# Two more pairs of tiles as seven block products, and input scaling and low parts moved to GpSimd, in a two-layer hybrid trunk

## The chip, the cores and the metric

The kernel runs on one core of a Trainium2 chip. The metric is device time in microseconds (us) from one launch; what is compared is the median of several runs. The profile names the engines PE (TensorE, with PEld for its weight loads), DVE (VectorE), ACT (ScalarE), POOL (GpSimd) and SP (SyncE, which here only issues DMA).

## The reference, cut to what matters

Two layers over 528 tokens (16 learned ones ahead of 512), width 1024, all in float32:

```
h = RMSNorm(x)
[u_pool | z_pool | c_q | c_kv | k_rope | z_mla | g_pool | g_mla] = h @ W_in
y_pool = (pool_mix(u_pool) * silu(z_pool)) @ W_pool_up
y_mla  = (attention(c_q, c_kv, k_rope) * silu(z_mla)) @ W_mla_up      8 heads, causal, q and k normalised, rotary part
x = x + (sigmoid(g_pool) * y_pool + sigmoid(g_mla) * y_mla) @ W_out
```

The 16 learned tokens are dropped at the end, so the second layer computes most things for 512 tokens only. The change touches, in the second layer, the columns of `W_in` that give `z_mla` (tiles `zm0` to `zm3`, 128 columns each), `g_pool` (`gp0` to `gp7`) and `g_mla` (`gm0` to `gm7`).

## The kernel before

**Precision.** Matmuls run in a reduced float32 format. To keep float32 accuracy each operand is split into a high part (ScalarE copies it into the reduced format) and a low part (VectorE subtracts the high part from the original). A product is three matmuls, `mm3`, lines 187 to 193: high by high (L188), high by low (L191), low by high (L192). `split`, lines 294 to 296, does it for activations; `wload`, lines 173 to 185, for weights, which come from HBM in chunks of 128 x 512 (K = 512 rows of a tile of 128 columns). A chunk costs a DMA on SP, an ACT copy (L183, `whi`) and a DVE subtraction (L184, `wlo`). There are three buffers each for the raw chunk, the high part and the low part.

**The stream.** `register` lists all weight products of both layers in order, as `Gemm` entries in `plan`; `stream` walks that list and yields after every few matmuls, with their nominal time. `clk` adds up these nominal times. `go` writes out the remaining work of a layer (norms, softmax, attention) and between its steps calls `fill`, `fill_now`, `fill_to` or `upto`, which take so many nominal nanoseconds of matmuls from the stream, or all up to a named entry. `after` puts a piece of work on a list that is run when `clk` has passed a given time. So the attention's small steps are covered by the stream's matmuls. In the second layer `gap` fills 2,700 nominal ns and stops at the entry in `RESERVE` ("gm5"), so that later entries are left to cover the end of the last head. The framework then orders each engine's instructions by a simulated timeline, so the order in the trace can differ from the program's.

**Block products.** `fast`, lines 599 to 646, computes two neighbouring tiles (a pair) as one 2 x 2 product of blocks: two halves of K by two tiles, times two halves of K by two halves of 256 tokens, with seven block products in place of eight (Winograd's form). Each of the seven is 4 k-steps x 3 matmuls of 256 columns. It needs sums of activation blocks, made by `mixed` (lines 577 to 597) on DVE and ACT once for all pairs, and sums of weight blocks, which `weight_sums` (lines 339 to 355) makes in the first layer: copies from HBM to HBM on SP's queue, additions by accumulating DMA on GpSimd's queue, four sums a pair, kept in `wsum`. The results come out of four PSUM banks through one ACT copy and five DVE additions or subtractions, then through `got_gp`, which applies the gate. Before, the four pairs of `gp` are made so.

**Plain entries.** `zm0` to `zm3` (`ev_zm`, lines 556 to 565) and `gm0` to `gm7` (`ev_gate`, lines 1029 to 1035) are plain: 8 k-steps x 3 matmuls of 512 columns. `ev_zm` makes one tanh on ACT and one instruction on DVE (L562), `ev_gate` one tanh; the gates `gm0` to `gm5` are stored to HBM and fetched again later.

**Input scaling.** `renorm`, lines 566 to 575, scales each of eight blocks of 128 rows of the layer's input by its gain and by the inverse norm (L573, on DVE), and splits it in place of the unscaled one. Blocks 0 to 3 are loaded from HBM first, since their buffer is in use. `qk_stats` calls it for the blocks in the order 4, 5, 6, 7, 0, 1, 2, 3, with 1,500 nominal ns of fill after each. `zm0` is the first entry that reads the scaled input.

**Heads.** For each of eight heads, `prep` (lines 840 to 860) multiplies keys by their inverse norm (DVE for one half, L847; GpSimd for the other, L848), splits keys (`kh`, `kl`) and queries (`qh`, `ql`, L854 and L855), and copies rotary parts by DMA. `head` computes scores, maxima (L877, DVE), exponentials (L884, ACT), and the normalisation by the row sums on GpSimd (L922, L924). `pv` transposes and multiplies by the values, one head later (L944 to L950). `go` calls `mixed` three times a head in the second layer, until its eight steps are done.

Of the kernel before, what the change touches and what calls it, by code (L numbers as in the profile page):

```python
# [53 lines left out]
RESERVE = ("gm5", "gm5")  # L54
# [4 lines left out]
SPACE = 4500.0  # L59
# [13 lines left out]
def trunk(ctx, tc, xT, pos, win, wkr, wqb, wkb, wvb, wgr, wpu, wmu, wout, gains, const, yT):  # L73
# [220 lines left out]
    def split(hi, lo, src, a, b):  # L294
        act.activation(hi[:, a:b], src, AF.Copy)  # L295
        dve.tensor_sub(lo[:, a:b], src, hi[:, a:b].bitcast(F32))  # L296
# [33 lines left out]
    wsum = [dp.tile([P, 4, 512], F32, name=f"wsum{u}") for u in range(4)]  # L330
# [8 lines left out]
    def weight_sums(w):  # L339
        def made(u, i):  # L340
            a, b = w[2 * u], w[2 * u + 1]
            d = wsum[u]
            src = {0: (b[:, 0:512], b[:, 512:1024]), 2: (a[:, 0:512], b[:, 0:512]), 1: (a[:, 0:512], d[:, 0, :]),
                   3: (a[:, 512:1024], d[:, 1, :])}
            return d[:, i, :], src[i]

        def copy(d, src):
            behind(sp.dma_start(d, src[0]), earlier(9000))

        def add(d, src):  # L350
            behind(gp.dma_start(d, src[1], accum_op=ALU.add), earlier(4000))

        for u in range(4):
            for fn, i in ((copy, 0), (copy, 2), (add, 0), (copy, 1), (add, 2), (add, 1), (copy, 3), (add, 3)):
                yield lambda fn=fn, u=u, i=i: fn(*made(u, i))

    class Layer:
        def __init__(self, l):
# [12 lines left out]
            self.f, self.tt, self.part = [None] * 8, [None] * 4, {}  # L371
            self.st = self.acc = self.inv = self.cinv = self.kraw = self.kp = None
# [193 lines left out]
        def renorm(self, k):  # L566
# [3 lines left out]
            if k < 4:  # L570
                sp.dma_start(f, scr[:, k, :])
                x = f
            behind(dve.scalar_tensor_tensor(out=f, in0=x, scalar=self.g(G_H + k), in1=self.inv[:, NM:T],  # L573
                                            op0=ALU.mult, op1=ALU.mult), newest[0])
# [24 lines left out]
        def fast(self, name, a, b, u, got):  # L599
# [4 lines left out]
            bank = {}  # L604

            def body(i, w):
# [21 lines left out]
                elif p == 5:  # L628
                    dve.tensor_sub(v, v, ps)
                    got(2 * u + 1, XH[1], v, v)  # L630
                elif p == 2:
                    got(2 * u, XH[0], ps, tmp()[:, :N2])
                elif p == 4:
                    x = tmp()[:, :N2]
                    dve.tensor_sub(x, ps, d)
                    got(2 * u + 1, XH[0], x, x)
                else:
                    dve.tensor_add(d, d, ps)
                    got(2 * u, XH[1], d, d)
# [6 lines left out]
        def got_gp(self, m, s, v, t):  # L646
            am = self.am[m][:, s[0]:s[1]]
            act.activation(t, v, AF.Tanh, scale=0.5)
            dve.scalar_tensor_tensor(out=am, in0=t, scalar=1.0, in1=am, op0=ALU.add, op1=ALU.mult)

# [154 lines left out]
        def qk_stats(self):  # L805
# [34 lines left out]
        def prep(self, h):  # L840
# [9 lines left out]
            split(kh, kl, kf[:, :T], 0, T)  # L850
# [4 lines left out]
            dve.tensor_sub(ql[n0:n0 + 64, x0:T], src, qh[n0:n0 + 64, x0:T].bitcast(F32))  # L855
# [218 lines left out]
        def register(self, nxt):  # L1074
# [46 lines left out]
            for m in range(4):  # L1121
                add(f"zm{m}", wi(MT_ZM + m), D, evac=self.ev_zm(m) if self.last else self.ev_silu(self.zms, "u", m),
                    xs=hs, segs=XS)
            if self.last:
                for e in ("gm0", "gm1", "gp0", "gm2", "gp1", "gm3", "gp2", "gm4", "gp3", "gm5", "gm6", "gm7"):
                    m = int(e[2])
                    if e[:2] == "gp":
                        self.fast(e, wi(MT_GP + 2 * m), wi(MT_GP + 2 * m + 1), m, self.got_gp)
                    else:
                        add(e, wi(MT_GM + m), D, evac=self.ev_gate(m), xs=hs, segs=XS)  # L1130
# [16 lines left out]
        def go(self, nxt):  # L1147
# [145 lines left out]
```

## Time and profile before

| | before |
|---|---|
| median of 3 runs | 788.73 us (788.3 to 789.17) |
| the profiled execution, whole | 788.28 us |
| its span, first to last instruction | 786.4 us |
| instructions | 15094 |
| granted TensorE clock | 1.000 of full speed |
| DMA, mean over the span | 124 GB/s |
| HBM read, written | 88.64 MB, 14.23 MB |

The profile is one execution. The page gives busy time by engine, the span in 40 slices with the busy share in tenths (9 is 90% or more), the chain of work that ended last, followed backwards from the last instruction, and groups of instructions: line, engine, operation, what is written and read, shapes, count, then busy time and mean nanoseconds of one, then idle time of the engine just before them and what ended it. A line like L184 is a line of the kernel. Matmuls overlap, so their durations add up to more than the time they take; starts are what to compare. Views of the trace give the same for a stretch of time (windows), for a line, or instruction by instruction (timeline: start, duration, engine, line, what).

### The profile page before, as it was taken

To read this page: it belongs to the slowest core of one execution; us is meant where nothing else is said; L and a number is where in the kernel's file an instruction comes from. 1 tells how busy PE (TensorE), PEld (TensorE's weight loads), DVE (VectorE), ACT (ScalarE), POOL (GpSimd) and SP (SyncE) were. 2 spreads that over 40 slices of the span, in tenths; PEclk is the share of its full clock that TensorE was granted. 3 is DMA by queue.
4 is the path that set the end of the run, shared out by engine and by line. 5 is a ranking of instruction groups with operands and counts; after the bars stand their busy time and mean duration, and the time that the engine had idled before them with its cause. 6 is when DMAs were issued, how large, how long until landed. Compare 5 with 4: busy or idle time off the path is not lost.

```text
span 786.4 us, 15094 instructions
## 1 busy us (share of the span) xinstructions
PE 778.8 (99%) x5445; PEld 713.4 (91%) x5445; DVE 558.8 (71%) x1229; ACT 427.1 (54%) x974; POOL 210.9 (27%) x275
## 2 busy tenths in 40 slices
PE   9999999999999999999999999999999999999998
PEld 8999899999999999999997898887778999887887
DVE  5848778447788977685355487775897899874932
ACT  8545655635656665643354455556657676654421
POOL 1034504002434342153000145122004323440600
PEclk9999999999999999999999999999999999999999
DMA  6242343434645435647742422435233454462372
GB/s 243 82 101 84 99 120 102 128 106 117 136 122 126 116 90 112 167 103 176 206 141 81 109 81 79 138 97 167 95 111 112 118 153 126 121 202 68 99 231 100
DMA packets 60907, 97.61 MB, mean 124 GB/s; under 512 B 9744, under 2 KB 18320, under 8 KB 60832
## 3 DMA queue, kind: packets, MB, share of 16 engines
q1 hardware_dynamic: 57520, 90.61, 38.8%
q0 software_dynamic: 2304, 4.20, 4.3%
q10 hardware_dynamic: 1008, 1.84, 0.7%
q8 instruction: 43, 0.70, 0.4%
q14 instruction: 32, 0.26, 0.1%
HBM read 88.64 MB, written 14.23 MB: 131 GB/s over the span
## 4 chain that ended last, share of the span: by engine, by line
PE 91%; DVE 4%; DMA 2%; issue 1%; ACT 1%; ACTq 0%; DVEq 0%
PE mm L188 27%; PE mm L192 27%; PE mm L191 26%; PE mm L944 2%; PE S L191 2%; PE S L192 2%; PE S L188 1%; DVE wlo L184 1%; PE o L950 1%; PE o L949 1%; PE S L498 1%; PE mm L400 1%; DMA xb<-xT 1%; DMA raw<-win 1%; DVE hl L296 0%
## 5 line engine op out<-in xcount | busy, mean ns | idle before, releaser
L188 PE MATMUL mm<-hh,whi 128*128 128x264 f32 (+2 forms) x1080 | 333.9, 311 | 0.1
L191 PE MATMUL mm<-hl,whi 128*128 128x264 f32 (+2 forms) x1080 | 332.5, 309 | 0.4 <-DVE hl L296 0.4
L192 PE MATMUL mm<-hh,wlo 128*128 128x264 f32 (+2 forms) x1080 | 332.1, 310 | 0.4 <-DVE wlo L184 0.4
L184 DVE TENSOR_TENSOR wlo<-raw,whi 128x512 fp32r<-128x512 f32 (+2 forms) x263 | 197.7, 756 | 108.8 <-ACT whi L183 105.3
L183 ACT ACTIVATE whi<-raw 128x512 fp32r<-128x512 f32 (+2 forms) x263 | 157.8, 603 | 179.3 <-PE mm L191 114.6
L188 PEld LDWEIGHTS mm<-hh,whi 128*128 128x128 f32 x1080 | 202.9, 188 | 11.8 <-ACT racc L958 0.5
L191 PEld LDWEIGHTS mm<-hl,whi 128*128 128x128 f32 x1080 | 203.3, 188 | 11.1 <-DVE hl L296 0.9
L192 PEld LDWEIGHTS mm<-hh,wlo 128*128 128x128 f32 x1080 | 202.5, 188 | 10.5 <-DVE wlo L184 1.1
L700 POOL TENSOR_TENSOR racc<-racc,tmp 128x264 f32<-128x264 f32 (+1 forms) x15 | 14.2, 950 | 144.2 <-ACT tmp L699 119.8
L192 PE MATMUL mm<-cq,wlo 128*128 128x264 f32 (+2 forms) x140 | 43.5, 313 | 0.6 <-DVE wlo L184 0.6
L188 PE MATMUL mm<-cq,whi 128*128 128x264 f32 (+2 forms) x140 | 44.0, 314 | 0.0
L191 PE MATMUL mm<-cq,whi 128*128 128x264 f32 (+2 forms) x140 | 43.4, 311 | 0.0
L848 POOL TENSOR_TENSOR tmp<-kp,bc 64x528 f32<-64x528 f32 x16 | 23.7, 1484 | 68.5 <-PE mm L815 44.4
L1049 POOL TENSOR_TENSOR tmp<-tmp,xb 128x264 f32<-128x264 f32 (+1 forms) x24 | 27.2, 1155 | 50.4 <-DVE tmp L1047 38.9
L877 DVE CUSTOM_DVE_ANT_0 S<-S,maskw,nqs 128x288 f32<-128x288 f32 (+4 forms) x80 | 38.3, 497 | 3.0 <-PE S L192 2.8
L922 POOL TENSOR_TENSOR pm<-pa,rs 128x16 f32<-128x16 f32 x32 | 10.9, 340 | 96.7 <-DVE rs L917 88.6
L188 PE MATMUL mm<-u,whi 128*128 128x264 f32 (+1 forms) x108 | 35.2, 326 | 0.1
L296 DVE TENSOR_TENSOR tl<-mm,th 128x512 fp32r<-128x512 f32 (+1 forms) x64 | 29.4, 481 | 7.7 <-ACT th L295 6.5
L192 PE MATMUL mm<-u,wlo 128*128 128x264 f32 (+1 forms) x108 | 34.7, 322 | 0.0
L924 POOL TENSOR_TENSOR cq<-cq,rs 128x384 f32<-128x384 f32 (+1 forms) x32 | 32.8, 1024 | 0.0
L191 PE MATMUL mm<-kn,whi 128*128 128x264 f32 (+1 forms) x96 | 30.6, 320 | 0.0
L188 PE MATMUL mm<-q,whi 128*128 128x264 f32 (+1 forms) x96 | 29.9, 323 | 0.6 <-ACT q L295 0.4
(309 smaller groups left out, 1472.3 us busy)
## 6 DMA issues: line engine op xcount, KB each, us to landing
raw<-win SPq DMA_DIRECT2D x139, 256.0 KB, 2.7
raw<-wout SPq DMA_DIRECT2D x32, 256.0 KB, 3.3
bc<-kdr SPq DMA_DIRECT2D x16, 264.0 KB, 4.1
raw<-wpu SPq DMA_DIRECT2D x16, 256.0 KB, 2.8
wsum<-win SPq DMA_DIRECT2D x16, 256.0 KB, 3.3
raw<-wmu SPq DMA_DIRECT2D x16, 256.0 KB, 2.8
raw<-wsum SPq DMA_DIRECT2D x16, 256.0 KB, 3.2
raw<-wqb SPq DMA_DIRECT2D x12, 256.0 KB, 2.6
```

Of the source, the lines that this page charges most:

```text
L183: act.activation(hi[:, :n], raw[:, :n], AF.Copy)
L184: dve.tensor_sub(lo[:, :n], raw[:, :n], hi[:, :n].bitcast(F32))
L188: first = pe.matmul(out, wh, xh, start=start, stop=False, skip_group_check=more)
L191: pe.matmul(out, wh, xl, start=False, stop=False, skip_group_check=more)
L192: newest[0] = pe.matmul(out, wl, xh, start=False, stop=stop, skip_group_check=more)
L296: dve.tensor_sub(lo[:, a:b], src, hi[:, a:b].bitcast(F32))
L700: self.acc_last = gp.tensor_add(self.acc[:, a:b], self.acc[:, a:b], t[:, :b - a])
L848: gp.tensor_mul(kf[r0:r0 + 64, :], self.kp[r0:r0 + 64, :], bc[r0:r0 + 64, :])
L877: dve.tensor_tensor_reduce(out=sv, in0=sv, in1=mask, scale=nqs[:, i, h:h + 1], scalar=3e38, op0=ALU.add, op1=ALU.min, accum_out=bia[:, c:c ...
L924: gp.tensor_mul(pt[i][:, NM:], pt[i][:, NM:], rs[:, i:i + 1].to_broadcast([P, n - NM]))
L944: pe.transpose(tr[:, P * (i - j):P * (i - j + 1)], pt[i][:, NM + P * j:NM + P * (j + 1)], ident)
L1049: gp.tensor_add(t[:, :b - a], t[:, :b - a], self.am[m][:, a:b])
```

## The change

In the second layer, `zm2` with `zm3` and `gm2` with `gm3` become block products too, so there are six pairs. The order of the entries after `zm1` is written out anew in `ORDER`; `RESERVE` names `gp67`. `weight_sums` makes sums for six pairs, one step every 4,000 nominal ns instead of 4,500. `renorm` multiplies by the inverse norm on GpSimd and applies the gain on ACT; blocks 4, 5 and 6 are scaled after `qn3`, ahead of `qk_stats`, and the other five inside it with 1,700 nominal ns of fill after each. In the second layer's `prep` the low parts of keys and queries are made on GpSimd. `mixed` is called four times a head. `fast` takes the numbers of its two tiles, and `got_zm` and `got_gm` finish the new pairs.

```diff
-RESERVE = ("gm5", "gm5")
+FAST = {"zm": MT_ZM, "gp": MT_GP, "gm": MT_GM}
+ORDER = "gm0 gm1 zm23 gp01 gm23 gp23 gm4 gp45 gm5 gp67 gm6 gm7"
+PAIRS = [(e[:2], int(e[2])) for e in ORDER.split() if len(e) == 4]
+RESERVE = ("gm5", "gp67")
...
-SPACE = 4500.0
+SPACE = 4000.0
...
-    def split(hi, lo, src, a, b):
+    def split(hi, lo, src, a, b, eng=dve):
         act.activation(hi[:, a:b], src, AF.Copy)
-        dve.tensor_sub(lo[:, a:b], src, hi[:, a:b].bitcast(F32))
+        eng.tensor_sub(lo[:, a:b], src, hi[:, a:b].bitcast(F32))
...
-    wsum = [dp.tile([P, 4, 512], F32, name=f"wsum{u}") for u in range(4)]
+    wsum = [dp.tile([P, 4, 512], F32, name=f"wsum{u}") for u in range(len(PAIRS))]
...
-        for u in range(4):
+        for u in range(len(w) // 2):
...
-            behind(dve.scalar_tensor_tensor(out=f, in0=x, scalar=self.g(G_H + k), in1=self.inv[:, NM:T],
-                                            op0=ALU.mult, op1=ALU.mult), newest[0])
+            behind(gp.tensor_mul(f, x, self.inv[:, NM:T]), newest[0])
+            act.activation(f, f, AF.Copy, scale=self.g(G_H + k))
             split(hh, hl, f, NM, T)
...
-        def fast(self, name, a, b, u, got):
+        def fast(self, name, a, b, u, ms, got):
...
+        def got_zm(self, m, s, v, t):
+            if self.zms[m] is None:
+                self.zms[m] = slot(f"u{m}")
+            t = tmp()[:, :N2]
+            act.activation(t, v, AF.Tanh, scale=0.5)
+            dve.scalar_tensor_tensor(out=self.zms[m][:, s[0]:s[1]], in0=t, scalar=1.0, in1=v,
+                                     op0=ALU.add, op1=ALU.mult)
+
+        def got_gm(self, m, s, v, t):
+            if self.gms[m] is None:
+                self.gms[m] = slot("ts" if m % 2 else "tc")
+            act.activation(self.gms[m][:, s[0]:s[1]], v, AF.Tanh, scale=0.5)
+            self.halves[m] += 1
+            if self.halves[m] == 2:
+                act.dma_start(gate[:, m, :], self.gms[m][:, NM:T])
...
-                for i, k in enumerate((4, 5, 6, 7, 0, 1, 2, 3)):
+                for i, k in enumerate((7, 0, 1, 2, 3)):
                     self.renorm(k)
-                    fill_to(start + 1500 * (i + 1))
+                    fill_to(start + 1700 * (i + 1))
...
-            split(kh, kl, kf[:, :T], 0, T)
+            rest = gp if self.last else dve
+            split(kh, kl, kf[:, :T], 0, T, rest)
...
-            dve.tensor_sub(ql[n0:n0 + 64, x0:T], src, qh[n0:n0 + 64, x0:T].bitcast(F32))
+            rest.tensor_sub(ql[n0:n0 + 64, x0:T], src, qh[n0:n0 + 64, x0:T].bitcast(F32))
...
-            for m in range(4):
+            for m in range(2 if self.last else 4):
                 add(f"zm{m}", wi(MT_ZM + m), D, evac=self.ev_zm(m) if self.last else self.ev_silu(self.zms, "u", m),
                     xs=hs, segs=XS)
             if self.last:
-                for e in ("gm0", "gm1", "gp0", "gm2", "gp1", "gm3", "gp2", "gm4", "gp3", "gm5", "gm6", "gm7"):
...
+                for e in ORDER.split():
...
             up("qn3")
+            if self.last:
+                for k in (4, 5, 6):
+                    self.renorm(k)
             self.qk_stats()
             if l == 0:
                 fill_now(2600)
-                for i, fn in enumerate(weight_sums([win[1, MT_GP + m] for m in range(8)])):
+                for i, fn in enumerate(weight_sums([win[1, FAST[t] + m + i] for t, m in PAIRS for i in range(2)])):
                     after(SPACE * (i + 1), fn)
...
                 self.gap()
+                self.mixed(next(mix))
                 self.mixed(next(mix))
```

More of the change, by code (lines that the diff above doesn't have):

```diff
@@ L629, in body @@
                     dve.tensor_sub(v, v, ps)
-                    got(2 * u + 1, XH[1], v, v)
+                    got(m1, XH[1], v, v)
                 elif p == 2:
-                    got(2 * u, XH[0], ps, tmp()[:, :N2])
+                    got(m0, XH[0], ps, None)
                 elif p == 4:
@@ L1124, in register @@
             if self.last:
[L1125 to L1130 removed]
+                got = dict(zm=self.got_zm, gp=self.got_gp, gm=self.got_gm)
+                for e in ORDER.split():
+                    t, m = e[:2], int(e[2])
+                    if len(e) == 3:
+                        add(e, wi(MT_GM + m), D, evac=self.ev_gate(m), xs=hs, segs=XS)
+                    else:
+                        w = wi(FAST[t] + m), wi(FAST[t] + m + 1)
+                        self.fast(e, *w, PAIRS.index((t, m)), (m, m + 1), got[t])
             else:
```

7 lines of the change are left out of this document (5 added, 2 removed).

## The prediction

> **What bounds the kernel now.** First the page's busy times, the slices and the chain.
>
> ```profile
> PE 778.8 (99%) x5445; PEld 713.4 (91%) x5445; DVE 558.8 (71%) x1229; ACT 427.1 (54%) x974; POOL 210.9 (27%) x275
> ...
> PE   9999999999999999999999999999999999999998
> ...
> DVE  5848778447788977685355487775897899874932
> ...
> POOL 1034504002434342153000145122004323440600
> ...
> PE 91%; DVE 4%; DMA 2%; issue 1%; ACT 1%; ACTq 0%; DVEq 0%
> ```
>
> TensorE is busy in every slice and holds 91% of the chain, so a matmul removed is time won, unless another engine then falls behind. The only near candidate is VectorE in slices 29 to 36 (from 560 to 700 us), which is the second layer from the input scaling to the last head, the stretch that the change rewrites. GpSimd is idle there more than half the time. I cut that stretch into windows (length, then busy time and count of PE, PEld, DVE, ACT, POOL, granted clock, DMA share, GB/s).
>
> ```profile
> 560.00:570.00 10.00, 10.00 (x45) 8.13 (x44) 9.97 (x25) 7.16 (x14) 0.00 (x0) 1.00 0.26 79
> 570.00:580.00 10.00, 9.15 (x44) 7.08 (x43) 10.00 (x30) 5.00 (x12) 0.00 (x0) 1.00 0.27 80
> ...
> 613.00:696.50 83.50, 82.62 (x592) 77.25 (x593) 78.29 (x181) 59.31 (x150) 31.39 (x44) 1.00 0.48 144
> ```
>
> TensorE stands still 0.85 us in 570 to 580 and 0.88 us in the stretch of block products (613 to 696.5, `gp0` to `gp3` with `gm2` to `gm4` between them); VectorE is at 100% and 94% there. The clock is granted in full. So there are two stocks: matmul time, and 1.7 us of standstill.
>
> **The products.** The distance between matmul starts is the price, not the duration, since they overlap. Two runs of 23 consecutive matmuls, first and last row of each (start, duration):
>
> ```profile
> 613.20 0.28 PE L191 MATMUL mm<-hl,whi 128*128 128x256 f32 x1
> ...
> 615.79 0.28 PE L192 MATMUL mm<-cq,wlo 128*128 128x256 f32 x1
> ...
> 628.69 0.39 PE L191 MATMUL mm<-hl,whi 128*128 128x512 f32 x1
> ...
> 633.77 0.40 PE L192 MATMUL mm<-hh,wlo 128*128 128x512 f32 x1
> ```
>
> (615.79-613.20)/22 = 0.118 us for 256 columns; (633.77-628.69)/22 = 0.231 us for 512. A plain pair of tiles is 2x8x3 = 48 matmuls, 11.1 us; a block product is 7x4x3 = 84, 9.9 us. Two pairs (`zm2`,`zm3` and `gm2`,`gm3`) save 2.4 us. If each of the 14 new weight chunks starts with a bubble as `gp0` did (0.1 us after a transpose), 1.0 us remain; I take 2.4, as the chunks behind the first one in these rows have none.
>
> **Scaling of the input.** The standstill at 570 to 580 comes from VectorE, which the chain (start, length) and the waits show:
>
> ```profile
> 557.96 0.68 DVE hl L296
> ...
> 562.04 0.67 DVE cq L573
> ...
> 570.72 0.60 DVE hl L296
> 572.10 0.61 DVE wlo L184
> 572.75 0.50 PE mm L192
> ...
> PE mm L191 <- DVE hl L296: 0.4, 1, 0.4
> ```
>
> `zm0` waits for the last scaled input. The change takes the eight multiplications at L573 from VectorE, brings three of the blocks forward to the end of `qn3`, and ends the other five after 6.8 us of planned fill instead of 10.5. In their place GpSimd multiplies eight times and ScalarE scales eight times:
>
> ```profile
> L573 DVE SCALAR_TENSOR_TENSOR cq<-xb,gn,rinv 128x512 f32<-128x512 f32 x3 | 2.2, 744 | 0.6 <-PE mm L192 0.6
> ...
> L700 POOL TENSOR_TENSOR racc<-racc,tmp 128x512 f32<-128x512 f32 x5 | 6.5, 1293 | 95.0 <-ACT tmp L699 95.0
> ...
> L295 ACT ACTIVATE hh<-cq 128x512 fp32r<-128x512 f32 x6 | 3.8, 628 | 2.0 <-DVE cq L573 2.0
> ```
>
> VectorE loses 8x0.74 = 5.9 us at its fullest place. GpSimd pays 8x1.3 = 10.3 us, where its slices are empty; ScalarE 8x0.63 = 5.0 us, at 5 to 7 of 10. The scaling of one block gets longer (1.3+0.63 in place of 0.74, so 1.2 us), less than the 3.7 us by which the last one starts earlier. The four loads from `scr` come earlier on SP with their blocks, among weight loads, at a DMA share of 0.26. A new wait stands on ScalarE: each scaling waits for GpSimd, and weight splits are queued behind it, on which TensorE depends. With three blocks in a row after `qn3` that is 3x(1.3-0.63), 2 us, against a plain chunk of 12x0.231 = 2.8 us that is split ahead. I take the 0.85 us as won; the bounds are this gain and, without that cover, a loss of 1.2 us (2 less 0.85).
>
> **VectorE in the block products.** Its added and removed work (the rows with x34 and x5 are of 613 to 696.5 alone, the others of the whole span):
>
> ```profile
> L184 DVE TENSOR_TENSOR wlo<-raw,whi x263: 282/692/1835, 6.1 to 775.2; 128x512 fp32r<-128x512 f32 x112, 128x256 fp32r<-128x256 f32 x16, 128x128 fp32r<-128x128 f32 x4
> ...
> L625 DVE TENSOR_TENSOR sv<-sv,mm 128x256 f32<-128x256 f32 x4 | 1.6, 410 | 0.0
> ...
> L649 DVE SCALAR_TENSOR_TENSOR xb<-sv,xb 128x256 f32<-128x256 f32 x8 | 3.7, 456 | 0.0
> ...
> L562 DVE SCALAR_TENSOR_TENSOR u<-tmp,mm x4: 670/678/681, 581.8 to 596.3; 128x512 f32<-128x512 f32 x4
> ...
> L184 DVE TENSOR_TENSOR wlo<-raw,whi 128x512 fp32r<-128x512 f32 x34 | 28.6, 840 | 1.7 <-ACT whi L183 1.4
> ...
> L296 DVE TENSOR_TENSOR kl<-tmp,kh 128x528 fp32r<-128x528 f32 x5 | 3.5, 699 | 1.7 <-ACT kh L295 1.7
> ...
> L855 DVE TENSOR_TENSOR qhl<-q,qhl 64x512 fp32r<-64x512 f32 x8 | 6.3, 786 | 0.1
> ```
>
> Added: three more weight chunks a pair, 6x0.69 = 4.1 us; five additions a pair, 10x0.41 = 4.1; for `zm` four gates of 0.46 in place of two of 0.68, +0.5; 8.7 us together. Removed: 8x(0.70+0.79) = 11.9 us of low parts of keys and queries, besides the 5.9. So in sum VectorE gets 9.1 us less, and ScalarE, idle 24 of the 83.5 us, takes six more weight splits and the two pairs' smaller activations, under 10 us.
>
> But four pairs now follow one another (`zm23 gp01 gm23 gp23`) where a plain `gm` tile stood after each. Load of these: a pair costs VectorE 7x0.69+5x0.41 = 6.9 us, and 1.8 more with gates, so 3x8.7+6.9 = 33.0. TensorE needs 39.6 us, and head work between: in today's stretch 82.6 less four pairs and three tiles (4x9.9+3x5.55 = 56.3) leaves 26.3 for five heads (`kl` x5), so 39.6 us of products come with 18.5 us, 3.5 heads, and 58.1 us on the clock. A head costs VectorE what is left of its 78.3 us after 34 weight chunks (34x0.69 = 23.5) and four pairs' additions and gates (4x3.9 = 15.6): 39.2/5 = 7.8 us, less the 1.5 moved, 6.3; 3.5 heads are 22.1. Sum 55.1 of 58.1 us, 95%, against 94% now. It fits, with 3.0 us to spare.
>
> **What GpSimd does to VectorE.** A subtraction next to a GpSimd instruction (start, duration):
>
> ```profile
> 558.33 1.52 POOL L848 TENSOR_TENSOR tmp<-kp,bc 64x528 f32<-64x528 f32 x1 [23.36 <-PE mm L815]
> ...
> 558.57 1.83 DVE L184 TENSOR_TENSOR wlo<-raw,whi 128x512 fp32r<-128x512 f32 x1
> ```
>
> 1.83 us where the median is 0.69: it ended 0.55 us after GpSimd did, so it was held 1.14 us. Over the stretch the 34 subtractions grew by 34x(0.84-0.69) = 5.1 us beside 31.4 us of GpSimd, 0.16 us per us. The moved low parts cost GpSimd about 1.3 us each (between 1.08 and 1.56 us, rows below), two a head: 7 in the dense part, 9 us, hence 1.5 us of growth inside the spare 3.0. For clumps I add 0.4 us; the bounds are 0 and 5.0 (7x1.14 less 3.0).
>
> The Trainium skill (SBUF — State Buffer, section "Who interferes with whom") says that a VectorE instruction with two SBUF inputs and a GpSimd one that reads SBUF exclude each other for the whole of the one that began first; the two rows above agree. By that rule taken at its full each moved low part can hold VectorE once for its whole length, which is the rival below.
>
> **Keys for the next head.** The low part must be there before the second matmul of the scores. One of the tightest heads:
>
> ```profile
> 674.19 0.65 ACT L295 ACTIVATE kh<-tmp 128x528 fp32r<-128x528 f32 x1 [2.04 <-POOL tmp L848]
> ...
> 674.87 0.71 DVE L296 TENSOR_TENSOR kl<-tmp,kh 128x528 fp32r<-128x528 f32 x1 [1.70 <-ACT kh L295]
> ...
> 676.66 0.37 PE L191 MATMUL S<-kl,qhl 128*128 128x272 f32 x1
> ...
> L924 POOL TENSOR_TENSOR cq<-cq,rs 128x512 f32<-128x512 f32 x16 | 17.2, 1078 | 0.0
> ...
> L1049 POOL TENSOR_TENSOR tmp<-tmp,xb 128x512 f32<-128x512 f32 x8 | 12.3, 1564 | 34.3 <-DVE tmp L1047 34.3
> ```
>
> `kh` ends at 674.84; on GpSimd `kl` would end at 675.9 to 676.4, still before 676.66. GpSimd's own queue holds the normalisations of the head before it, but these come ahead of the key product L848, which `kh` awaits anyhow. While GpSimd waits for `kh`, the next normalisations (L922, L924) stand behind it; the value products need these only in the following head. I put the cost at 0; if the queries' low part stands in front it is up to 1.3-0.3 = 1.0 us a head, 7 us for seven heads.
>
> **The rest, at nothing.** Mixing the operands (four steps a head instead of three) ended at 584.7 and `zm23` starts where `zm3` ends today, after 596.3: 11 us of cover. The sums of weights grow by eight transfers on SP's queue and eight on GpSimd's, in the first layer:
>
> ```profile
> L296 DVE TENSOR_TENSOR cq<-sv,cq x1: 672/672/672, 584.1 to 584.1; 128x512 fp32r<-128x512 f32 x1
> ...
> L351 POOL DMA_DIRECT2D wsum<-win x8 | 6.7, 839 | 56.7 <-PE mm L192 56.7
> ...
> SPq L348 <- PE mm L192: 18.7, 9, 3.8
> ```
>
> GpSimd has room for 8x0.84 us. On SP the 16 copies waited nine times for a matmul, at most 3.8 us, with weight loads queued behind; no TensorE wait came of it. Without that cover, one such wait less a chunk's 2.8 us (12x0.231) would be 1.0 us. The reserve for the last head stays `gm6` and `gm7`.
>
> **Sum.** -2.4-0.85+0.4 = -2.85 us on 788.28 (span 786.4 and 1.9 around it): 785.4. The median of the runs is 0.45 above the profiled one, so 785.9.
>
> **Rivals.** *VectorE is held by GpSimd (slower).* Place: `zm23` to `gp23`. Each of the seven moved low parts holds VectorE 1.14 us, 8.0 against 3.0 spare, so TensorE stands 5.0 us: 788.73-2.4-0.85+5.0 = 790.5. It is slower than now from 0.89 us an instruction ((3.0+3.25)/7). For it: the row of 1.83 us and 95% load. Against: the mean growth of 0.16 per us.
> *The keys come late.* GpSimd is slow or in the wrong order in the heads, 0.3 us in each of eight, and the scaling's 0.85 us is not won: 788.73-2.4+2.4 = 788.7. For it: 0.2 to 0.7 us of margin at 676. Against: VectorE let `kl` wait for a turn in other heads, GpSimd need not.
> *Relief beyond the count.* VectorE's 9.1 us less also end the 0.88 us in the stretch: 788.73-2.4-0.85-0.88 = 784.6.
>
> **How the numbers follow.** Forecast 0.52 (own range 784.9 to 787.1), relief 0.14, late keys 0.16, VectorE held 0.18. A measurement tells about 0.2%, 1.6 us, from no change, so faster is below 787.15. Forecast and relief make 0.66; late keys lie within (0.15) but for a hundredth; of the held case 0.16 is slower and 0.02 within. Faster 0.67, same 0.17, slower 0.16. The range 784.2 to 790.2 leaves out the low edge of relief and most of the held case.
>
> **What would show it.** Right: no TensorE idle at 570 to 580; 168 more 256-column matmuls and 96 fewer of 512; VectorE below 95% between the first and last block product; `kl` ending before the scores need it. Wrong: TensorE idle before an L192 that awaits `wlo`, VectorE subtractions over 0.84 us in the mean, or scores waiting for POOL.

## The result and the profile after

| | before | changed |
|---|---|---|
| median | 788.95 us (788.3 to 791.68, 6 runs) | 794.22 us (793.12 to 796.4, 6 runs) |
| ratio | 1 | 1.0066, 95% interval 1.0046 to 1.0085 |
| the profiled execution, its span | 788.28, 786.4 us | 794.89, 793.1 us |
| instructions | 15094 | 15360 |

The kernel became slower by 5.3 us; the forecast was 785.9, and the range ended at 790.2. The page of the changed kernel has the same three readings as the page of before (in its lines L191, L194 and L195 are the three matmuls of `mm3`, L186 and L187 are `whi` and `wlo`, L298 and L299 the `split`):

```profile
PE 778.6 (98%) x5517; PEld 717.5 (90%) x5517; DVE 565.3 (71%) x1223; ACT 436.1 (55%) x994; POOL 251.3 (32%) x307
...
PE   9999999999999999999999999999999889999998
...
PE 87%; DVE 6%; issue 2%; ACT 1%; DMA 1%; POOL 1%; DVEq 0%; ACTq 0%; POOLq 0%
```

TensorE has 72 matmuls more, 168 of 256 columns less 96 of 512, as counted. It is busy as long as before (778.6 and 778.8 us), but it stands still 14.5 us of the span (793.1-778.6) where it stood 7.6 (786.4-778.8). The 6.9 us between them cover the 6.7 by which the span grew. Besides the last slice, two more show 8 now, from 615 to 654 us. Windows of the changed kernel (length, then busy time and count of PE, PEld, DVE, ACT, POOL, granted clock, DMA share, GB/s) put the standstill in place:

```profile
570.00:580.00 10.00, 10.00 (x47) 8.24 (x47) 10.00 (x25) 6.45 (x15) 3.20 (x2) 1.00 0.31 94
580.00:590.00 10.00, 8.37 (x39) 6.68 (x39) 9.48 (x23) 5.80 (x16) 5.29 (x4) 1.00 0.34 100
...
600.00:610.00 10.00, 8.79 (x70) 8.16 (x69) 8.14 (x24) 8.45 (x24) 5.97 (x10) 1.00 0.40 119
...
630.00:640.00 10.00, 8.17 (x62) 7.79 (x63) 10.00 (x29) 6.21 (x19) 2.21 (x2) 1.00 0.50 141
640.00:650.00 10.00, 7.00 (x61) 6.79 (x60) 9.11 (x20) 7.60 (x22) 9.77 (x17) 1.00 0.52 138
650.00:660.00 10.00, 9.95 (x69) 9.58 (x67) 6.19 (x13) 5.11 (x11) 4.02 (x3) 0.83 0.48 146
...
601.30:708.00 106.70, 100.11 (x751) 95.34 (x751) 94.37 (x216) 72.79 (x185) 45.08 (x60) 0.98 0.47 138
```

The standstill at 570 to 580 is gone, as forecast. In its place come others, mainly four: in 580 to 590, 600 to 610, 630 to 640 and 640 to 650, and from 650 to 660 the granted clock is 0.83. The last row is the stretch of all the block products: VectorE is busy 94.37 of 106.70 us, 88%, and TensorE still misses 6.6 us there. So VectorE had room in the sum, and what was late was late at single moments. The waits of TensorE (us in total, times, longest):

```profile
PE mm L978 <- DVE pmr L961: 3.0, 1, 3.0
PE mm L195 <- DVE wlo L187: 2.5, 3, 1.6
PE o L973 <- DVE tl L299: 2.3, 1, 2.3
```

The timeline (start, duration, engine, line, what; in brackets the idle time before and what ended it) around the first and the third of the standstills by time:

```profile
582.81 1.40 POOL L299 TENSOR_TENSOR kl<-tmp,kh 128x528 fp32r<-128x528 f32 x1 [1.83 <-ACT kh L298]
...
582.97 1.79 DVE L187 TENSOR_TENSOR wlo<-raw,whi 128x512 fp32r<-128x512 f32 x1
...
584.80 0.50 PE L195 MATMUL mm<-hh,wlo 128*128 128x512 f32 x1 [1.63 <-DVE wlo L187]
...
627.85 1.32 POOL L870 TENSOR_TENSOR tmp<-kp,bc 64x528 f32<-64x528 f32 x1 [6.63 <-PE S L195]
...
628.01 1.71 DVE L187 TENSOR_TENSOR wlo<-raw,whi 128x512 fp32r<-128x512 f32 x1
...
629.61 1.26 POOL L878 TENSOR_TENSOR qhl<-q,qhl 64x512 fp32r<-64x512 f32 x1 [0.44 <-ACT qhl L877]
629.65 1.51 DVE L655 SCALAR_TENSOR_TENSOR xb<-tmp,xb 128x256 f32<-128x256 f32 x1
...
631.08 0.68 DVE L299 TENSOR_TENSOR tl<-mm,th 128x512 fp32r<-128x512 f32 x1
...
631.81 0.50 PE L973 MATMUL o<-tl,vt 128*128 128x512 f32 x1 [2.31 <-DVE tl L299]
```

At 582.81 the low part of the keys, now on GpSimd, holds the weight subtraction beside it for 1.79 us, where the median of these is 0.69, and TensorE waits 1.63 us. At 628 to 631 two VectorE instructions in a row are held, one by the key product and one by the queries' low part, and the `tl` that TensorE needs comes last in the queue. And at 646:

```profile
644.66 1.30 POOL L878 TENSOR_TENSOR qhl<-q,qhl 64x512 fp32r<-64x512 f32 x1
...
645.93 0.73 POOL L945 TENSOR_TENSOR pm<-pa,rs 128x16 f32<-128x16 f32 x1
...
647.23 2.19 DVE L961 TENSOR_TENSOR pmr<-pm,pmr 128x128 fp32r<-128x128 f32 x1
...
649.57 0.53 PE L978 MATMUL mm<-identr,pmr 128*96 128x128 f32 x4 [3.00 <-DVE pmr L961]
```

The normalisation `pm` stands behind the queries' low part on GpSimd; the subtraction that follows it, L961, takes 2.19 us beside further normalisations, and TensorE stands 3.00 us. Read alone, these rows say that GpSimd holds VectorE: the slower rival of the prediction. The experiments had to say whether that is where 5.3 us come from.

The page says one thing more: VectorE is busy 6.5 us longer than before (565.3 and 558.8), where the prediction had 9.1 us less.

For all kernels I add up three parts of the span. **Standstill**: the distance between the starts of two consecutive matmuls less what the columns of the first one need (columns x 0.417 ns + 10 ns, at least 60 ns; this gives 0.117 us for 256 and 0.223 for 512, beside 0.118 and 0.231 in the prediction's rows), counted where over 0.15 us is left; where the granted clock is 0.5, the need counts double. **Half clock**: half the time in which the granted clock is 0.5. **The rest**: the span less these two, which is matmul time. Before has 9.4, 0 and 777.1 us; the changed kernel 16.4, 1.7 and 775.0. So the products did win 2.1 us (2.4 were forecast), and standstill and half clock took 8.7. All these parts are of one execution of each kernel, and executions of one kernel differ: the 60 of the kernel before that ran beside the experiments took 786.93 to 794.83 us.

### The profile page after: what moved, and what is told of

It reads as the page before. It is cut to its first block, busy times and chain, and to the rows that moved or that the text cites. A ratio compares the mean times of both kernels' runs of the same rounds, so it can differ in the third digit from the quotient of the medians.

```text
span 793.1 us, 15360 instructions
## 1 busy us (share of the span) xinstructions
PE 778.6 (98%) x5517; PEld 717.5 (90%) x5517; DVE 565.3 (71%) x1223; ACT 436.1 (55%) x994; POOL 251.3 (32%) x307
## 4 chain that ended last, share of the span: by engine, by line
PE 87%; DVE 6%; issue 2%; ACT 1%; DMA 1%; POOL 1%; DVEq 0%; ACTq 0%; POOLq 0%
PE mm L191 26%; PE mm L195 26%; PE mm L194 26%; DVE wlo L187 2%; PE mm L967 2%; PE S L194 1%; PE S L195 1%; PE o L973 1%; PE S L191 1%; PE o L972 1%; PE S L502 1%; DVE S L900 1%; DVE tmp L869 1%; DMA xb<-xT 1%; PE mm L404 1%
## 5 line engine op out<-in xcount | busy, mean ns | idle before, releaser
L191 PE MATMUL mm<-hh,whi 128*128 128x264 f32 (+2 forms) x1072 | 328.7, 308 | 1.0 <-ACT whi L186 0.9
L195 PE MATMUL mm<-hh,wlo 128*128 128x264 f32 (+2 forms) x1072 | 326.4, 307 | 1.9 <-DVE wlo L187 1.9
L194 PE MATMUL mm<-hl,whi 128*128 128x264 f32 (+2 forms) x1072 | 326.4, 305 | 0.0
L187 DVE TENSOR_TENSOR wlo<-raw,whi 128x512 fp32r<-128x512 f32 (+2 forms) x269 | 208.8, 779 | 113.2 <-ACT whi L186 106.2
L186 ACT ACTIVATE whi<-raw 128x512 fp32r<-128x512 f32 (+2 forms) x269 | 161.4, 603 | 168.8 <-PE mm L194 116.0
L191 PEld LDWEIGHTS mm<-hh,whi 128*128 128x128 f32 x1072 | 201.6, 189 | 11.4 <-ACT whi L186 1.3
L195 PEld LDWEIGHTS mm<-hh,wlo 128*128 128x128 f32 x1072 | 201.2, 188 | 10.6 <-DVE wlo L187 2.3
L194 PEld LDWEIGHTS mm<-hl,whi 128*128 128x128 f32 x1072 | 202.0, 188 | 9.0
L191 PE MATMUL mm<-cq,whi 128*128 128x264 f32 (+2 forms) x156 | 49.1, 315 | 0.0
L195 PE MATMUL mm<-cq,wlo 128*128 128x264 f32 (+2 forms) x156 | 48.5, 312 | 0.6 <-DVE wlo L187 0.6
L194 PE MATMUL mm<-cq,whi 128*128 128x264 f32 (+2 forms) x156 | 48.3, 311 | 0.0
L722 POOL TENSOR_TENSOR racc<-racc,tmp 128x264 f32<-128x264 f32 (+1 forms) x15 | 14.2, 950 | 88.0 <-ACT tmp L721 63.8
L900 DVE CUSTOM_DVE_ANT_0 S<-S,maskw,nqs 128x272 f32<-128x272 f32 (+4 forms) x80 | 38.7, 497 | 3.1 <-PE S L195 2.8
L354 POOL DMA_DIRECT2D wsum<-win x12 | 10.0, 846 | 95.0 <-PE mm L195 93.0
L191 PE MATMUL mm<-u,whi 128*128 128x264 f32 (+1 forms) x108 | 35.2, 326 | 0.0
L195 PE MATMUL mm<-u,wlo 128*128 128x264 f32 (+1 forms) x108 | 34.7, 322 | 0.0
L907 ACT ACTIVATE cq<-S,bia 128x400 f32<-128x400 f32 (+2 forms) x48 | 24.5, 514 | 18.2 <-DVE bia L935 9.8
L299 DVE TENSOR_TENSOR tl<-mm,th 128x512 fp32r<-128x512 f32 (+1 forms) x64 | 29.6, 481 | 6.3 <-ACT th L298 6.2
L195 PEld LDWEIGHTS mm<-cq,wlo 128*128 128x128 f32 x156 | 29.8, 191 | 2.6 <-DVE wlo L187 1.0
```

Source lines behind the costliest of these rows:

```text
L186: act.activation(hi[:, :n], raw[:, :n], AF.Copy)
L187: dve.tensor_sub(lo[:, :n], raw[:, :n], hi[:, :n].bitcast(F32))
L191: first = pe.matmul(out, wh, xh, start=start, stop=False, skip_group_check=more)
L194: pe.matmul(out, wh, xl, start=False, stop=False, skip_group_check=more)
L195: newest[0] = pe.matmul(out, wl, xh, start=False, stop=stop, skip_group_check=more)
L299: eng.tensor_sub(lo[:, a:b], src, hi[:, a:b].bitcast(F32))
```

## The experiments

All ratios are to the kernel before, run on the same chip in the same job; in brackets stands the 95% interval.

**Moves and pairs apart.** The theories were H, that the moved low parts and scalings hold VectorE, and D, that four products in a row are too dense. Two kernels are the changed one with one move undone (the low parts; the scaling, again one VectorE instruction, at the change's places), one is before with both moves and the change's places of the scaling, and one is the changed kernel with both moves undone:

```diff
 e1 (changed kernel)
-            rest = gp if self.last else dve
+            rest = dve
 e2 (changed kernel)
-            behind(gp.tensor_mul(f, x, self.inv[:, NM:T]), newest[0])
-            act.activation(f, f, AF.Copy, scale=self.g(G_H + k))
+            behind(dve.scalar_tensor_tensor(out=f, in0=x, scalar=self.g(G_H + k), in1=self.inv[:, NM:T],
+                                            op0=ALU.mult, op1=ALU.mult), newest[0])
 e4 = e1 and e2 together; e3 = the kernel before with the opposite of both
```

> The changed kernel (median 794.2 us) with the low parts of keys and queries back on VectorE; pairs and scaling stay as changed. Theory H (GpSimd's moved low parts hold VectorE, which then is late with wlo and tl): the standstills at 582, 629 and 646 us go, 786 to 789 us. Rival D (four pairs in a row load VectorE beyond the clock, whoever makes the low parts): VectorE gets 12 us more work, so slower than the changed kernel, 796 us or more. Rival Q (GpSimd's queue: low parts stand in front of a head's normalisations): as H for the 646 standstill alone, 790 us.

> The changed kernel with the input scaling back in one VectorE instruction, at its new place in the program; pairs and low parts stay as changed. Theory H says that what costs is the low parts, so 793 to 796 us, with standstills in the heads as before. Rival S (the scaling on GpSimd and ScalarE is what delays the heads): 788 to 790 us. Rival D: 794 to 796 us.

> The kernel before with only the two moves to GpSimd (scaling, low parts) and the new places of the scaling; four pairs as before. Theory H: slower than before by the holds alone, 790 to 793 us, and TensorE standstills of 2 us or more in the heads. Rival D: VectorE has 17 us less work and no denser products, so at least as fast as before, 786 to 788.5 us.

> The changed kernel with both moves undone: six pairs, new order, scaling and low parts on VectorE. Theory H: the pairs' 2.4 us are won, less some load on VectorE: 786 to 790 us. Rival D: VectorE carries 17 us more than in the changed kernel in the same stretch: 797 us or more.

Measured: low parts back on VectorE 1.0051 [1.0034, 1.0067], 792.73 us; scaling back 1.0087 [1.0056, 1.0118], 795.63; both moves on the four pairs of before 1.0025 [1.0013, 1.0038], 790.88; six pairs without any move 1.0056 [1.0033, 1.0079], 793.65. H has the second and the third within its ranges, but misses the first and the last; D misses all but the second. The last one decides against H as the main cause: without a move the kernel is nearly as slow as the changed one. Its waits:

```profile
PE S L191 <- ACT cq L907: 2.4, 3, 1.2
...
PE o L973 <- DVE tl L299: 0.9, 3, 0.4
PE mm L191 <- DVE u L545: 0.8, 1, 0.8
PE mm L191 <- DVE sv L643: 0.7, 1, 0.7
PE mm L195 <- DVE wlo L187: 0.6, 1, 0.6
```

None of the three waits of the changed kernel is there in its size. Others are, on ScalarE above all, and the sum is much the same: standstill and half clock 19.0 us, against 18.1. The holds of GpSimd are real: the wait of 1.6 us for `wlo` between 583 and 586 is there in the changed kernel and, as the next rows show, with both moves on four pairs, and in neither of the two kernels with the low parts on VectorE (e1 and e4); with the scaling back on VectorE (e2) it is gone too. The waits of e3 begin so:

```profile
PE mm L192 <- DVE wlo L184: 2.6, 3, 1.6
PE mm L188 <- ACT q L295: 1.4, 1, 1.4
```

But taking the low parts off GpSimd gains 0.15% of the time, 1.2 us, which the two intervals do not tell from nothing, and taking the scaling off gains nothing, as new waits stand elsewhere.

Undoing a move also gives VectorE its work back, so this does not say that the holds are harmless. The busy times of six pairs without the moves (e4) and of the moves on four pairs (e3) show what the moves were worth to VectorE:

```profile
PE 781.4 (98%) x5517; PEld 719.1 (91%) x5517; DVE 566.2 (71%) x1247; ACT 431.0 (54%) x986; POOL 216.7 (27%) x283
PE 778.1 (98%) x5445; PEld 713.3 (90%) x5445; DVE 557.8 (71%) x1205; ACT 431.9 (55%) x982; POOL 246.6 (31%) x299
```

By the prediction's count the moves take 17.8 us from VectorE (11.9 and 5.9). Its busy time fell by 0.9 us with six pairs (566.2 to 565.3) and by 1.0 with four (558.8 to 557.8). The rest, some 17 us, came back as longer VectorE instructions. The subtraction L961 is one of them: its four calls in the second layer take 277 to 284 ns without the moves and up to 2189 ns with them.

```profile
L961 DVE TENSOR_TENSOR pmr<-pm,pmr x4: 277/278/284, 599.9 to 710.8; 128x128 fp32r<-128x128 f32 x4
L961 DVE TENSOR_TENSOR pmr<-pm,pmr x4: 278/529/2189, 599.7 to 710.7; 128x128 fp32r<-128x128 f32 x4
```

**Fewer dense stretches.** Theory O was the order of the entries: a plain tile behind each pair should end the loss. `s1_spread` reorders and lets `mixed` run earlier, the second one also puts the low parts back, the third is before with the scaling alone on GpSimd, and the fourth has only one new pair, `gm23`.

```diff
-ORDER = "gm0 gm1 zm23 gp01 gm23 gp23 gm4 gp45 gm5 gp67 gm6 gm7"
+ORDER = "gm0 zm23 gm1 gp01 gm4 gp23 gm5 gp45 gm23 gp67 gm6 gm7"
...
-                kn_ = self.head(h, kq, prev, lambda: self.mixed(next(mix)))
+                kn_ = self.head(h, kq, prev, lambda: [self.mixed(next(mix)) for _ in range(4)])
```

> The changed kernel (794.2 us) with another order of its entries: gm0 zm23 gm1 gp01 gm4 gp23 gm5 gp45 gm23 gp67 gm6 gm7, so that the first four pairs have a plain tile ahead of each (the operands are mixed earlier in the program for it). Same work on every engine. Theory O (four pairs in a row leave VectorE no plain tile in which to catch up, and TensorE then stands still and loses its clock): 788 to 791 us, no granted clock of one half in the heads. Rival N (each further pair costs its weight chunks and additions wherever it stands): 793 to 795 us, and the standstills move along with the pairs.

> The spread order and the low parts of keys and queries back on VectorE; scaling on GpSimd. Theory O, with the low parts' cost of about 1.5 to 2 us as measured in the first four runs: 1.5 us below the spread order alone, 786.5 to 789 us. Rival N: 792 to 793.5 us.

> The kernel before with the scaling moved (GpSimd and ScalarE, earlier) and nothing else. If the scaling is worth the 1 to 1.4 us by which its undoing lengthened the changed kernel, and the low parts cost 1.5 to 2 us: 787 to 788.5 us. If the moves alone lost their 1.9 us through the scaling: 790 to 791 us.

> The changed kernel with gm23 as the only new pair (zm2 and zm3 plain, ahead of gm0), order gm0 gm1 gp01 gm4 gp23 gm5 gp45 gm23 gp67 gm6 gm7. Theory O: the first two pairs have plain tiles between, the last three stand in a row where VectorE had room: 789 to 791 us. Rival N (about 2.3 us for each new pair net of what it saves): 791.5 to 792.5 us.

Measured: 1.0126 [1.0111, 1.0141], 797.67 us; 1.0101 [1.0086, 1.0116], 795.48; 1.0053 [1.0036, 1.007], 792.23; 1.0081 [1.0066, 1.0097], 794.56. No range of either theory holds any of the four. Spreading (with the earlier mixing that it needs) made it worse, and five pairs are no better than six. The scaling alone (1.0053) is no faster than the scaling together with the low parts (1.0025): effects of single edits do not add. That points to a cause that every edit shares, whatever its work.

**Edits without work.** What every edit shares is that the framework orders each engine's instructions anew by its simulated timeline. Theory P blamed the places of the scaling, theory T the new order as such. Four kernels: before with the scaling at the change's places (on VectorE still); before with another number of nominal nanoseconds of fill in a gap, twice; and the changed kernel with the scaling back at the old places and `mixed` earlier as in `s1_spread`.

```diff
 n1: before, blocks 4, 5, 6 after qn3, the others every 1700 (n4: the reverse, on the changed kernel)
-                for i, k in enumerate((4, 5, 6, 7, 0, 1, 2, 3)):
+                for i, k in enumerate((7, 0, 1, 2, 3)):
 n2, n3: before
-FILL = (2950.0, 2700.0)
+FILL = (2950.0, 2650.0)    (n3: 2725.0)
```

> The kernel before with the scaling at its new places (blocks 4, 5, 6 after qn3, then five at 1,700 ns) and still on VectorE; nothing else changed, the same work on every engine. All eight runs with the new places so far were slower than before. Theory P (the places: the heads start about 7 us earlier, onto a VectorE that is still full with scaling and mixing): 791 to 793 us. Rival T (no one part, the order of before is a tuned one and any shift costs): 789.5 to 793 us too, told apart by the next three. Neither: 788 us.

> The kernel before with 2,650 in place of 2,700 nominal ns of fill in each gap between a head's steps of the second layer: the same work, nothing moved to another engine, 1.6 us of matmuls shifted over all heads. Theory T: slower by 1.5 to 4 us, 789.5 to 792 us, with new standstills in the heads. Rival P: within 1 us of before, 787 to 789 us.

> The kernel before with 2,725 nominal ns of fill in each gap, half the shift of the last one, to the other side. Theory T: 789.5 to 792 us. Rival P: 787 to 789 us.

> The changed kernel (794.2 us) with the scaling at its old places (all eight blocks inside qk_stats, 1,500 ns each), still on GpSimd and ScalarE, six pairs and low parts as changed; the operands' mixing is called earlier in the program. Theory P: the places' cost is gone, 787 to 790 us. Rival T, or the pairs themselves: 792 us or more.

Measured: 1.0131 [1.0095, 1.0167], 797.87 us; 1.0143 [1.0125, 1.0161], 798.97; 1.0072 [1.0057, 1.0087], 793.38; 1.0226 [1.0204, 1.0248], 804.68. P falls: the fill alone costs as much as the places, and the old places are the slowest of all. T has the direction right in all four, but its ranges for the first three were too low. A fill of 2650 in place of 2700, with as many instructions on every engine (5445 matmuls, 1229 on VectorE, 974 on ScalarE, 275 on GpSimd), costs twice what the change costs. What differs is the order: compare the two sequences of matmuls (line, operands and shape, by their starts), and 146 of the 5445 have to be taken out of one so that what is left stands in the other in the same order. Two windows of this kernel and two of its waits:

```profile
670.00:680.00 10.00, 7.42 (x60) 7.01 (x58) 9.46 (x26) 5.87 (x17) 5.13 (x8) 0.96 0.51 147
680.00:690.00 10.00, 9.88 (x38) 8.10 (x39) 6.60 (x14) 4.70 (x13) 5.86 (x9) 0.70 0.20 64
```

```profile
PE o L949 <- ACT th L295: 2.4, 1, 2.4
PE o L949 <- DVE tmp L965: 1.8, 1, 1.8
```

and the timeline where the 2.4 us arise:

```profile
677.28 0.66 POOL L922 TENSOR_TENSOR pm<-cq,rs 128x16 f32<-128x16 f32 x1
...
677.97 0.31 ACT L937 ACTIVATE pmr<-pm 128x128 fp32r<-128x128 f32 x1 [1.59 <-POOL pm L922]
...
678.53 0.61 ACT L183 ACTIVATE whi<-raw 128x512 fp32r<-128x512 f32 x1
679.05 0.26 ACT L295 ACTIVATE th<-mm 128x128 fp32r<-128x128 f32 x1
...
679.36 0.48 PE L949 MATMUL o<-th,vt 128*128 128x128 f32 x1 [2.41 <-ACT th L295]
```

In this order the split `th` that TensorE needs comes on ScalarE behind `pmr`, which waits 1.59 us for GpSimd's normalisation, and TensorE waits with it. This is a standstill as long as those of the changed kernel, with no part of the change in it.

**Neighbours of both kernels.** If the order is what costs, the changed kernel must be compared with before over several orders. Both at 2650, 2675, 2710 and 2725 nominal ns (before at 2650 and 2725 are the two above), same edit:

> The changed kernel with 2,650 nominal ns in each gap of the second layer's heads, nothing else. Theory T (the planned order decides; the change's 2.4 us of matmuls are real but smaller than what one plan differs from the next): anywhere from 787 to 800 us, at least 2 us from the changed kernel's 794.2. Rival W (the changed kernel's work as such costs 5 us, VectorE and GpSimd in each other's way): within 1.5 us of 794.2.

> The same at 2,675 ns. Theory T: 787 to 800 us, and not between the times at 2,650 and 2,700 except by chance. Rival W: within 1.5 us of 794.2.

> The same at 2,725 ns. Theory T: 787 to 800 us; if the changed kernel has a good plan anywhere near, one of these three is below the kernel before, 787 us or less. Rival W: within 1.5 us of 794.2.

> The kernel before at 2,675 ns, between its 2,700 (788) and 2,650 (799.0). Theory T: 790 to 799 us; the times of the kernel before at 2,650, 2,675 and 2,725 against the changed kernel's at the same three then say what the change does to a plan that was not chosen for it: with the matmuls real, the changed kernel's mean is not above. A smooth dependence on the fill: 793 us, half way.

> The changed kernel with 2710 nominal ns of fill in a gap in place of 2700; the work is the same. If the time is set mainly by the planned order: a draw from 0.5 to 1.5% over the kernel before, not tied to the 0.66% of 2700. If six pairs cost a fixed loss beside the products that they save: 0.66% again, within 0.2.

> The kernel before with 2710 nominal ns of fill in place of 2700. If the order of before is a favourable one among its neighbours: 0.5 to 1.5% slower than at 2700. If the kernel before is as fast at any order, and only 2650, 2675 and 2725 happened to be bad: within 0.2% of it. For the pair: if the denser products have a loss of their own as large as the result, the changed kernel is slower than this one by 0.5% or more; if they have none, it is faster by about 0.25% in the mean over the four fills, with a scatter of 0.5% in each.

The ratio, then standstill and half clock in us, then how many matmuls stand out of the sequence of the same kernel at 2700, counted as above:

| fill | before | | | changed | | |
|---|---|---|---|---|---|---|
| 2650 | 1.0143 [1.0125, 1.0161] | 16.2 + 3.4 | 146 | 1.01 [1.0062, 1.0137] | 17.5 + 3.4 | 193 |
| 2675 | 1.0083 [1.0055, 1.0111] | 14.2 + 1.7 | 121 | 1.0107 [1.0085, 1.0129] | 18.4 + 1.7 | 130 |
| 2700 | 1 | 9.4 + 0 | | 1.0066 [1.0046, 1.0085] | 16.4 + 1.7 | |
| 2710 | 1.0037 [1.0015, 1.0059] | 13.8 + 0 | 51 | 1.0058 [1.0035, 1.0082] | 16.4 + 1.7 | 57 |
| 2725 | 1.0072 [1.0057, 1.0087] | 14.1 + 1.7 | 119 | 1.012 [1.0095, 1.0145] | 18.8 + 3.4 | 91 |

Before at 2700 is the fastest of its row of five, by 0.37% to 1.43%, and has the least standstill of all 20 kernels profiled here (9.4 us; the next has 13.2). In this row the loss grows with the distance of the order: 0.37, 0.72, 0.83 and 1.43% for 51, 119, 121 and 146. So 2710, the nearest, which lay between its two expectations, keeps part of the lead. It is no rule: the changed kernel, compared with itself at 2700, loses most at 2725 with 91 out of sequence, and n1, with 282, loses less than before at 2650. The changed kernel at 2710 has the ratio of 2700 again (both of its expectations allow that), and its wait of 3.0 us for L961:

```profile
PE mm L978 <- DVE pmr L961: 3.0, 1, 3.0
PE mm L195 <- DVE wlo L187: 2.6, 3, 1.6
PE o L973 <- DVE tl L299: 1.5, 1, 1.5
```

The times at 2650, 2675 and 2725 (796.26, 797.52 and 798.26 us) lie outside the 1.5 us of rival W, and none is below the kernel before. Without 2700, the changed kernel is slower than before at the same fill by -0.43, +0.24, +0.21 and +0.48%, in the mean 0.13%, 1.0 us, with a scatter that does not tell it from nothing. Its standstill with half clock, in one execution of each, is longer in all four pairs, by 1.3, 4.2, 4.3 and 6.4 us, in the mean 4.0.

The matmul time, in contrast, is nearly the same in every order. Of the eight kernels with four pairs the rest of the span is 776.4 to 778.2 us, of the eleven with six pairs 773.8 to 775.7, and with five 776.2; the means of the first two are 777.0 and 774.8. So the products of two pairs are worth 2.1 us.

## Why the prediction was wrong

**The terms that held.** The products: 2.1 us of the 2.4 forecast, by the counted instructions. The standstill of `zm0`: TensorE is busy for 10.00 of 10.00 us at 570 to 580. The reason given was only half of it, though: before with nothing but the places moved (n1) also shows 10.00 there,

```profile
570.00:580.00 10.00, 10.00 (x51) 8.47 (x50) 10.00 (x28) 7.44 (x16) 0.00 (x0) 1.00 0.31 86
```

so the earlier places win the 0.85 us, and GpSimd's multiplication was not needed for it. VectorE's load where four pairs follow one another (601.3 to 666.0 us): busy 56.49 us, where 55.1 and 1.5 of growth were worked out. Weight sums and keys at nothing: no wait of TensorE for either stands among the waits of the second layer.

**The step that failed** is "For clumps I add 0.4 us; the bounds are 0 and 5.0". It took the price of the new stretch from VectorE's load, the 3.0 us to spare, and let the standstill of before (1.7 us in two places) stand for what such a load leaves. In its place the runs showed +7.0 us of standstill and 1.7 of half clock, outside both bounds. The four pairs took 64.70 us where 58.1 were worked out, and TensorE was idle for 6.58 of them, though VectorE had 8.2 us to spare. The rows are the changed kernel, then the same four pairs with both moves undone (e4):

```profile
601.30:666.00 64.70, 58.12 (x455) 56.13 (x455) 56.49 (x127) 44.34 (x111) 28.01 (x35) 0.97 0.47 136
604.30:664.40 60.10, 58.16 (x453) 56.15 (x452) 53.57 (x131) 41.78 (x110) 18.32 (x28) 0.97 0.50 138
```

The step ahead of it, that "in sum VectorE gets 9.1 us less", failed too: it got 6.5 more. The pairs cost it 7.4 (558.8 to 566.2), near the 8.7 worked out, but the moves gave back 0.9 and not 17.8.

By the table, the 8.7 can be written as a sum of three; this is bookkeeping on one execution of each kernel, and not three causes shown apart:

- The low 9.4 us of before belong to its one order, not to its load. Its four neighbours with the same work have 13.8 to 19.6, in the mean 16.3 (half clock included), 6.9 more. All 19 other kernels here stand still for longer, 13.2 us or more; the prediction should have had it as a cost of its own. The changed kernel at 2700 is better than its neighbours too, 18.1 against their mean of 20.3, so 2.2 came back.
- The change brings standstill of its own, 4.0 us in the mean of the four pairs of neighbours. The sum is 6.9-2.2+4.0 = 8.7. The 4.0 rests on four pairs only, from 1.3 to 6.4, which does not tell it from the 2.1 that the products save; the ratios of these pairs do not either (0.13% in the mean).

The rival of 790.5, VectorE held by GpSimd, has the place right and nearly the size, but not the whole time:

- The holds by GpSimd are in the rows (1.79 and 1.71 us where 0.69 is the median). The rule of the Trainium skill that was cited (SBUF — State Buffer, section "Who interferes with whom") agrees with these rows. What the holds add up to is large: 16.9 us of VectorE's relief lost (17.8 less 0.9) beside 34.6 us more of GpSimd (216.7 to 251.3) is 0.49 us per us, where the prediction took 0.16 from the weight subtractions alone.
- At the place that the rival names, `zm23` to `gp23`, TensorE is idle for 6.58 us (the rival has 5.0), and for 4.2 to 6.8 in all seven kernels that keep this order of entries with the low parts on GpSimd. With the low parts on VectorE it is 2.71 (e1) and 1.94 (e4).
- Yet the whole time does not follow: without the low parts on GpSimd the ratio is 1.0051, without either move 1.0056. Those kernels stand still elsewhere. So the holds decide where the changed kernel stands still, and not, as far as these runs show, how long in all.
- The sign that the prediction named for this rival, 0.84 us in the mean for the subtractions, is not reached in the stretch of block products, where before has 840 ns without any move. That mean was a poor sign: from 543 us on the same 89 subtractions take 856 ns with the moves and 773 without (e4). The row of the stretch:

```profile
L187 DVE TENSOR_TENSOR wlo<-raw,whi 128x512 fp32r<-128x512 f32 x44 | 36.4, 826 | 3.6 <-ACT whi L186 2.9
```

**The range** was too narrow for the same reason: its bounds were those of the terms, and a change of the order, which lengthened before by 0.4 to 1.4% with no work changed, was not among them.

**What stays open.** Why the order of before is so good was not found; no one wait explains it, as the longest waits of the slow neighbours differ from one to the next. Whether the 4.0 us come from the pairs or from the moves was not taken apart over several orders; at 2700 the pairs without the moves have 15.6 + 3.4, and VectorE is as busy with them as with the moves (566.2 and 565.3). That this unrelieved load is what makes the changed kernel's orders worse fits these figures and is not shown. Nor does a run show how the order of before was found, so that it was selected for its time is a guess. None of the 18 other kernels beats before; whether the changed one would at some other fill or spacing was tried at four other fills only.

## What to carry to other kernels

In a kernel whose instruction order is planned by a simulated timeline, the time is work plus the standstill of one particular plan, and the plan at hand can be a low value among its neighbours: before pricing an edit, give the neighbours of the kernel as it stands (a fill a little longer and shorter) to the chip, and put their spread into the range. Judge an edit by pairs at several such settings and not by one, and when a profile shows a convincing culprit, remove it alone: here each culprit could be removed, and others took its place. Before counting work that is moved to GpSimd as relief for VectorE, compare VectorE's busy time with and without the move: here 17.8 us of moved work freed 0.9. A matmul saved on a TensorE that is 99% busy is won only as far as the engines that feed it are early at every single moment; a sum of their load over 60 us does not show that.

## What the runs showed of the hardware

After the standstill at 646 the granted clock halves, for 3.4 us. Windows of the changed kernel ahead of it, in it and behind it:

```profile
646.20:651.20 5.00, 1.95 (x15) 1.44 (x14) 4.97 (x6) 2.40 (x5) 5.00 (x9) 1.00 0.41 111
651.30:654.60 3.30, 3.30 (x17) 3.30 (x17) 1.94 (x4) 1.43 (x3) 1.98 (x2) 0.50 0.65 225
654.70:665.00 10.30, 10.30 (x85) 10.16 (x85) 7.86 (x20) 6.42 (x15) 1.97 (x2) 1.00 0.35 103
```

The starts of matmuls of 256 columns in it, first and last of fifteen:

```profile
651.41 0.41 PE L194 MATMUL mm<-hl,whi 128*128 128x256 f32 x1
...
654.40 0.41 PE L191 MATMUL mm<-cq,whi 128*128 128x256 f32 x1
```

They stand (654.40-651.41)/14 = 0.214 us apart, where 0.118 is usual; over 3.4 us the loss is 1.5 us (1.7 by the measure of half the time), about half of the standstill that came before it, and it comes while TensorE has work. At a fill of 2650 the window is twice as long (the row of 680 to 690 above, clock 0.70). The profiled execution of before does not show it; of the 60 others beside the experiments, 8 have a mean granted clock of 0.996 to 0.998, as the changed kernel has with its one window (0.998). In the profiles, all nine standstills above 2.5 us by the measure used here were followed by it within 1.7 us, or it began before they ended (2.62 us in before at 2650, 2.82 in n1, 2.91 in the changed kernel at 2675, 3.05 to 3.24 in five kernels, 4.34 in the changed one at 2725), and so were three of 0.92, 0.88 and 0.67 us within 3 us (e1). Of shorter ones some were and some were not: 1.78 us (n4) was, 1.82 (e3) was not, and of three between 2.42 and 2.48 us one was. The Trainium skill (TensorE: Matmul & The Clock Gate, section "HAM oscillation — how this bites in real kernels") puts the limit at gaps of TensorE above some 3.4 us; here less was enough. A standstill of over 2.5 us can thus cost some 1.5 us more than its length.
